# Final x by token: turned in quarters beside the second feed-forward's output products, its place lent to four raw weight buffers

## The chip, the core and the metric

The kernel runs on one core of one Trainium2 chip. The time is device microseconds (us) of one launch. Engines in the rows: PE is TensorE, DVE VectorE, ACT ScalarE, POOL GpSimd, and SP the engine whose queue issues nearly all loads.

## The reference

One encoder layer over 256 tokens of width D = 2048, in float32: two feed-forwards of width F = 5632 around a mixer and a cross-attention, and a last RMSNorm:

```python
x = x + 0.5 * swiglu_ffn(rms_norm(x, ffn1_norm), ffn1_w_in, ffn1_w_out)
...
x = x + memory_cross_attention(h, mem_n, w_q, w_kv, w_o)
x = x + 0.5 * swiglu_ffn(rms_norm(x, ffn2_norm), ffn2_w_in, ffn2_w_out)
return rms_norm(x, final_norm)          # swiglu_ffn: (silu(h @ gate) * (h @ up)) @ w_out
```

## The kernel before

**Precision and weights.** A product in float32 is made of three matmuls on a high and a low part of each operand. A weight block of 128 x 1024 floats (512 KB) is loaded by SP into a raw buffer; ACT casts it to its high part, DVE subtracts to get the low part, and PE uses both. In the feed-forward's input products ACT's cast is L341 and DVE's subtraction L342 (`parts`); elsewhere they are L112 and L113 (`weights`). The two parts of a block live in one of five places in turn (three tiles `hl`, two of `ring`), so ACT and DVE can be at most five blocks ahead of PE there, and three ahead elsewhere.

**Input products of a feed-forward (`FeedForward`, L299).** The hidden width is cut into 11 groups of 512. Group 0 is plain: 16 blocks k, each with 12 matmuls (`by_two`, L279). Groups 1 to 10 (`group`, L423) take the 16 blocks in 8 pairs: "S" pairs save one of eight products by sums of blocks (`seven`, L381, whose sums are DVE's L387, L388, L393 and L400), "C" pairs are plain (`eight`). Three blocks of a group (k = 2, 7, 13) have their low part made by an accumulating DMA that POOL issues (`summed`, L354, tile `hl_s`) instead of by DVE. At the end of a group DVE adds up what is in PSUM (L452), and `give` (L414) makes silu(gate) * up: ACT's L417, then DVE's L419. ACT's L417 therefore marks the end of each group in the trace.

**Raw buffers.** `raw` (L347) takes them in turn: four of the pool `wraw`, then those in the list `raws`. In the first feed-forward `raws` has five places, all in the tile `spare`: nine buffers in all. In the second, the first half of `spare` is `x2`, the place of the final x by token, so `raws` has one place and there are five buffers. DVE turns x (`xT`, by feature) into `x2` with 32 transpositions of 32 x 512 elements (`turn`, L973 to L981; DVE's L978), which are put on a list and issued behind DVE's subtractions during groups 0 to 2: `put(cost, ...)` appends to the list, `beside(per)` issues from it until a budget is spent. Before group 3 `then` is called (L471): it issues what is left, and four raw buffers are opened in the place of `xT`, which nobody needs any longer. From there on the second feed-forward has nine buffers too.

**Output products (`gemm_n`, L160).** The output is made in four quarters of 512 columns, each in 22 steps. A step takes one raw buffer and is 12 matmuls (L171 to L173: two blocks k, two token tiles, three matmuls each). During the first quarter the hidden tiles are also turned (`turns`, PE's L263, ACT's L120, DVE's L121). After each quarter `add_up` (L1009) adds half of the product to `x2`, and POOL multiplies by the last norm's gain; the last quarter and the norm follow at L1047 to L1074.

**What sets the order.** Within an engine a scheduler orders the instructions by a model of their times when the program is built; every engine then works its own list strictly in order, and SP's list of loads likewise. A load waits until its buffer has been read by all readers of its last contents: ACT, DVE, and for a `summed` block the DMA that POOL issued.

Of the kernel before, what the change touches and what calls it, by code (L numbers as in the profile page):

```python
# [17 lines left out]
P = 128  # L18
# [48 lines left out]
def layer(ctx: ExitStack, tc: tile.TileContext, a: dict):  # L67
# [231 lines left out]
    class FeedForward:  # L299
# [6 lines left out]
        def __init__(self, stack, tags, x_hl, gain, w_in, pattern):  # L306
# [18 lines left out]
            self.sums = spare[:, 4096:5120]  # L325
            self.raws = [spare[:, 5120:6144]]
            if tags[0] == "S1":
                self.raws += [spare[:, i * 1024:(i + 1) * 1024] for i in range(4)]
            self.raw_at = 0
# [92 lines left out]

        def group(self, j, r, per, after=()):  # L423
            b = {}
# [9 lines left out]
            for p, c in enumerate(self.pattern):  # L434
# [8 lines left out]
                else:  # L443
                    late = p > self.spairs[-1] and len(after) > 0
                    self.eight(j, p, b, p == self.pattern.index("C"), p == n - 1, late)
                    if p > self.spairs[-1] + 1:
                        for _ in range(2):
                            if after:
                                after.pop(0)()
                beside(per)  # L450
            for acc, u in (("2", p1), ("4", u2), ("3", u4), ("8", u5)):
                nc.vector.tensor_tensor(out=u, in0=u, in1=b[acc], op=ALU.add)  # L452
            self.give(j, (p1, u2), (u4, u5), r)

        def run(self, before, after, root, then, per):
            acc = token_accs()
            self.sums_at = [(j, k) for j in range(1, NG) for k in SUMMED if j < NG - 1 or k < SUMMED[-1]]
            for k in range(KD):
                before(k)
                w = self.parts(self.raw(0, k))  # L460
                begin = [(t, g) for t in range(2) for g in range(2)] if k == 0 else []
                by_two(acc, self.x_hl[:, k], w[:, 0], w[:, 1], k, begin, k == KD - 1)
                after(k)
                if k == 13:
                    r = root()
                    nc.scalar.activation(out=st.tile([P, 1], F32, name="warm"), in_=ones[:, 0:1], func=AF.Silu)
                    self.summed(*self.sums_at[0])
            self.give(0, [acc[t][0] for t in range(2)], [acc[t][1] for t in range(2)], r)
            turns = [self.turn(i) for i in range(2 * NG)]
            for j in range(1, NG):  # L470
                if j == 3:  # L471
                    then()
                if j < NG - 1:
                    self.group(j, r, per)
                else:
                    now, turns = turns[:4], turns[4:]
                    self.group(j, r, per, now)
            return turns
# [46 lines left out]
    with ExitStack() as stack:  # L525
# [21 lines left out]

        turns = ff.run(x_arrives, x_more, x_root, lambda: None, 0.0)

# [419 lines left out]
    with ExitStack() as stack:  # L969
        ff = FeedForward(stack, ("S0", "S1", "S2"), x_hl, "ffn2_norm", a["ffn2_w_in"], PATTERNS[1])  # L970
        x2 = ff.x2

        def turn(i, j):  # L973

            def go():
                q = j % 4
                dst = x2[32 * q:32 * q + 32, j // 4].rearrange("p (f n) -> p f n", n=P)
                nc.vector.transpose(  # L978
                    out=dst[:, :, 32 * i:32 * i + 32], in_=xT[32 * i:32 * i + 32, :, 32 * j:32 * j + 32]
                )  # L980
            return go  # L981

        h = ff.of
        put(0.6, *[turn(i, j) for i in range(4) for j in range(8)])

        def first_beside(k):
            if k in (6, 9, 12):
                ff.sides(k // 3 - 2)
            beside(0.8)

        def x_turned():
            finish()
            raws = xt.tile([P, 4, 1024], F32, name="raws", tag="x")
            ff.raws += [raws[:, i] for i in range(4)]

        turns = ff.run(lambda k: None, first_beside, lambda: rms_cols(ss, D, "r_x2"), x_turned, 0.6)
        finish()
        acc_0 = gemm_n(a["ffn2_w_out"][0], h, between=turns, after=0)
        ff.high.close()
# [39 lines left out]
        for n in range(3):  # L1039
            acc = gemm_n(a["ffn2_w_out"][n], h) if n else acc_0  # L1040
            for t in range(2):
                add_up(t, slice(n * 512, (n + 1) * 512), acc[t], n)


# [92 lines left out]
```

## Time and profile before

| | us |
|---|---|
| median of 3 runs (lowest, highest) | 2136.71 (2135.22, 2139.54) |
| the profiled execution, its own time | 2133.17 |
| its span, first to last instruction | 2131.4 |
| granted TensorE clock, mean of the span | 0.995 |

Times in rows are counted from the start of the span. The first feed-forward's input products take the span's first 480 us, the second's lie from 1388 to 1872 us, and its output products from 1872 us to the end. A row of the timeline gives start, duration, engine, line, operation, what it writes and reads, and in brackets for how long its engine sat idle before it and what ended that; "SPq" is SP's queue of loads, where the duration runs from the first issue to the last.

### The profile page before, as it was taken

To read this page: it belongs to the slowest core of one execution; us is meant where nothing else is said; L and a number is where in the kernel's file an instruction comes from. 1 tells how busy PE (TensorE), PEld (TensorE's weight loads), DVE (VectorE), ACT (ScalarE), POOL (GpSimd) and SP (SyncE) were. 2 spreads that over 40 slices of the span, in tenths; PEclk is the share of its full clock that TensorE was granted. 3 is DMA by queue.
4 is the path that set the end of the run, shared out by engine and by line. 5 is a ranking of instruction groups with operands and counts; after the bars stand their busy time and mean duration, and the time that the engine had idled before them with its cause. 6 is when DMAs were issued, how large, how long until landed. Compare 5 with 4: busy or idle time off the path is not lost. (4 is left out here: it accounts for less than half of the span.)

```text
span 2131.4 us, 26548 instructions
## 1 busy us (share of the span) xinstructions
PE 2091.1 (98%) x9764; PEld 1739.2 (82%) x9764; DVE 1559.3 (73%) x2119; ACT 1153.5 (54%) x1450; POOL 63.9 (3%) x81
## 2 busy tenths in 40 slices
PE   8999999999999999999999999998999999999998
PEld 6887888888888888888888888886788778888886
DVE  6887888776655589888877666797777888765444
ACT  7655566555544454445754455554565566554443
POOL 0000000000000000000000000000000000000000
PEclk9999999999999999999999999999999999999999
DMA  9787778855766766666655544566788778656664
GB/s 349 218 240 227 240 236 242 254 159 169 220 191 188 222 223 201 180 186 180 187 193 185 185 153 129 192 201 195 238 242 236 232 233 257 188 157 203 191 194 149
DMA packets 121954, 440.23 MB, mean 207 GB/s; under 512 B 13664, under 2 KB 13792, under 8 KB 121696
## 3 DMA queue, kind: packets, MB, share of 16 engines
q1 hardware_dynamic: 113184, 407.35, 59.6%
q0 software_dynamic: 8352, 30.41, 7.7%
q8 instruction: 76, 1.25, 0.2%
q10 hardware_dynamic: 288, 0.79, 0.1%
q14 instruction: 54, 0.44, 0.1%
HBM read 405.99 MB, written 2.10 MB: 191 GB/s over the span
## 5 line engine op out<-in xcount | busy, mean ns | idle before, releaser
L113 DVE TENSOR_TENSOR hl<-raw,hl 128x1024 fp32r<-128x1024 f32 (+1 forms) x402 | 489.8, 1219 | 322.1 <-ACT hl L112 321.2
L112 ACT CAST hl<-raw 128x1024 fp32r<-128x1024 f32 (+1 forms) x402 | 419.5, 1045 | 485.9 <-PE acc L173 299.7
L288 PE MATMUL acc<-hl,x_hl 128*128 128x512 f32 x440 | 151.6, 395 | 15.1 <-ACT hl L341 15.1
L341 ACT CAST hl<-spare 128x1024 fp32r<-128x1024 f32 (+1 forms) x105 | 102.8, 999 | 107.5 <-DVE spare L388 69.3
L342 DVE TENSOR_TENSOR hl<-raw,hl 128x1024 fp32r<-128x1024 f32 (+1 forms) x115 | 130.2, 1137 | 40.1 <-ACT hl L341 39.7
L289 PE MATMUL acc<-hl,x_hl 128*128 128x512 f32 x440 | 158.3, 395 | 0.1
L341 ACT CAST hl<-raw 128x1024 fp32r<-128x1024 f32 (+1 forms) x115 | 111.3, 981 | 71.6 <-DVE raw L400 40.8
L291 PE MATMUL acc<-hl,x_hl 128*128 128x512 f32 x440 | 137.9, 393 | 0.0
L342 DVE TENSOR_TENSOR hl<-spare,hl 128x1024 fp32r<-128x1024 f32 (+1 forms) x105 | 120.7, 1159 | 21.2 <-ACT hl L341 21.0
L341 ACT CAST ring<-spare 128x1024 fp32r<-128x1024 f32 (+1 forms) x75 | 74.1, 996 | 68.7 <-DVE spare L388 43.5
L288 PEld LDWEIGHTS acc<-hl,x_hl 128*128 128x128 f32 x440 | 83.5, 191 | 33.2 <-ACT hl L341 15.9
L172 PE MATMUL acc<-hl,x_hl 128*128 128x512 f32 x256 | 100.5, 392 | 0.1
L172 PE MATMUL acc<-hl,m_hl 128*128 128x512 f32 x256 | 100.3, 392 | 0.0
L173 PE MATMUL acc<-hl,m_hl 128*128 128x512 f32 x256 | 100.2, 391 | 0.0
L173 PE MATMUL acc<-hl,x_hl 128*128 128x512 f32 x256 | 99.8, 390 | 0.0
L289 PEld LDWEIGHTS acc<-hl,x_hl 128*128 128x128 f32 x440 | 83.3, 190 | 18.6 <-DVE hl L342 1.5
L291 PEld LDWEIGHTS acc<-hl,x_hl 128*128 128x128 f32 x440 | 83.7, 190 | 17.7
L342 DVE TENSOR_TENSOR ring<-spare,ring 128x1024 fp32r<-128x1024 f32 (+1 forms) x75 | 86.3, 1156 | 11.4 <-ACT ring L341 11.4
L289 PE MATMUL acc<-ring,x_hl 128*128 128x512 f32 x256 | 92.0, 390 | 2.1 <-DVE ring L342 2.1
L289 PE MATMUL acc<-hl_s,x_hl 128*128 128x512 f32 x232 | 89.3, 390 | 2.2 <-DMA hl_s<-raw 1.7
L171 PE MATMUL acc<-hl,m_hl 128*128 128x512 f32 x256 | 91.2, 392 | 0.0
L125 PE MATMUL acc<-x_hl,hl 128*128 128x512 f32 x256 | 91.0, 398 | 0.0
(343 smaller groups left out, 5185.4 us busy)
## 6 DMA issues: line engine op xcount, KB each, us to landing
raw<-in_ffn_w_in SPq DMA_DIRECT2D x176, 512.0 KB, 4.8
raw<-in_ffn_w_out SPq DMA_DIRECT2D x176, 512.0 KB, 3.8
spare<-in_ffn_w_in SPq DMA_DIRECT2D x120, 512.0 KB, 5.1
raws<-in_ffn_w_in SPq DMA_DIRECT2D x56, 512.0 KB, 5.1
raw<-in_w_mix_vg SPq DMA_DIRECT2D x32, 512.0 KB, 4.6
raw<-in_w_k SPq DMA_DIRECT2D x32, 512.0 KB, 3.9
raw<-in_w_v SPq DMA_DIRECT2D x32, 512.0 KB, 4.3
raw<-in_w_mix_out SPq DMA_DIRECT2D x32, 512.0 KB, 3.8
```

Source lines behind the costliest of these rows:

```text
L112: nc.scalar.copy(out=hl[:, 0, :size], in_=raw[:, :size])
L113: newest[0] = nc.vector.tensor_tensor(out=hl[:, 1, :size], in0=raw[:, :size], in1=hl[:, 0, :size].bitcast(F32), op=ALU.subtract)
L125: nc.tensor.matmul(acc, lhsT=w_hi, rhs=x_hl, start=first, stop=False, skip_group_check=True)
L171: nc.tensor.matmul(acc[t], lhsT=x[:, 0, s], rhs=hi[:, k], start=k0 + k == 0, stop=False)
L172: nc.tensor.matmul(acc[t], lhsT=x[:, 0, s], rhs=lo[:, k], start=False, stop=False)
L173: nc.tensor.matmul(acc[t], lhsT=x[:, 1, s], rhs=hi[:, k], start=False, stop=k0 + k == nk - 1)
L288: nc.tensor.matmul(acc[t][g], lhsT=x[:, 0, s], rhs=hi[:, cols[g]], start=(t, g) in first, stop=False)
L289: nc.tensor.matmul(acc[t][g], lhsT=x[:, 0, s], rhs=lo[:, cols[g]], start=False, stop=False)
L291: nc.tensor.matmul(acc[t][g], lhsT=x[:, 1, s], rhs=hi[:, cols[g]], start=False, stop=last)
L341: nc.scalar.copy(out=hl[:, 0, :n], in_=raw[:, :n])
L342: newest[0] = nc.vector.tensor_tensor(out=hl[:, 1, :n], in0=raw[:, :n], in1=hl[:, 0, :n].bitcast(F32), op=ALU.subtract)
```

## The change

The final x by token is no longer turned during groups 0 to 2 of the second feed-forward but during its output products, in four quarters of 512 columns: 32 transpositions of 32 x 128 elements per quarter. The first quarter's go behind the steps of the first quarter of the output, the other 96 behind the steps of the second and third. The first half of `spare` holds four raw buffers from group 0 on in both feed-forwards, and the four in the place of `xT` are gone. The calls of `beside` in the groups go with it.

```diff
@@ -323,9 +323,7 @@
             self.x2 = spare[:, :4096].rearrange("p (t d) -> p t d", t=2)
             self.free = spare[:, 4096:]
             self.sums = spare[:, 4096:5120]
-            self.raws = [spare[:, 5120:6144]]
-            if tags[0] == "S1":
-                self.raws += [spare[:, i * 1024:(i + 1) * 1024] for i in range(4)]
+            self.raws = [spare[:, i * 1024:(i + 1) * 1024] for i in (5, 0, 1, 2, 3)]
             self.raw_at = 0
...
@@ -420,7 +418,7 @@
-        def group(self, j, r, per, after=()):
+        def group(self, j, r, after=()):
...
                         for _ in range(2):
                             if after:
                                 after.pop(0)()
-                beside(per)
...
-        def run(self, before, after, root, then, per):
+        def run(self, before, after, root):
...
             for j in range(1, NG):
-                if j == 3:
-                    then()
                 if j < NG - 1:
-                    self.group(j, r, per)
+                    self.group(j, r)
...
@@ -970,32 +965,26 @@
-        def turn(i, j):
+        def turn(n, i, j):
 
             def go():
                 q = j % 4
-                dst = x2[32 * q:32 * q + 32, j // 4].rearrange("p (f n) -> p f n", n=P)
+                dst = x2[32 * q:32 * q + 32, j // 4, n * 512:(n + 1) * 512].rearrange("p (f n) -> p f n", n=P)
                 nc.vector.transpose(
-                    out=dst[:, :, 32 * i:32 * i + 32], in_=xT[32 * i:32 * i + 32, :, 32 * j:32 * j + 32]
+                    out=dst[:, :, 32 * i:32 * i + 32],
+                    in_=xT[32 * i:32 * i + 32, 4 * n:4 * n + 4, 32 * j:32 * j + 32],
                 )
             return go
 
         h = ff.of
-        put(0.6, *[turn(i, j) for i in range(4) for j in range(8)])
-
         def first_beside(k):
             if k in (6, 9, 12):
                 ff.sides(k // 3 - 2)
-            beside(0.8)
-
-        def x_turned():
-            finish()
-            raws = xt.tile([P, 4, 1024], F32, name="raws", tag="x")
-            ff.raws += [raws[:, i] for i in range(4)]
-
-        turns = ff.run(lambda k: None, first_beside, lambda: rms_cols(ss, D, "r_x2"), x_turned, 0.6)
+
+        turns = ff.run(lambda k: None, first_beside, lambda: rms_cols(ss, D, "r_x2"))
+        put(0.3, *[turn(0, i, j) for i in range(4) for j in range(8)])
+        acc_0 = gemm_n(a["ffn2_w_out"][0], h, per=0.55, between=turns, after=0)
         finish()
-        acc_0 = gemm_n(a["ffn2_w_out"][0], h, between=turns, after=0)
         ff.high.close()
...
         for n in range(3):
-            acc = gemm_n(a["ffn2_w_out"][n], h) if n else acc_0
+            if n == 1:
+                put(0.3, *[turn(m, i, j) for m in range(1, 4) for i in range(4) for j in range(8)])
+            acc = gemm_n(a["ffn2_w_out"][n], h, per=0.75) if n else acc_0
             for t in range(2):
                 add_up(t, slice(n * 512, (n + 1) * 512), acc[t], n)
+        finish()
```

Engine orders follow, the rows of each program apart; the changed program's line numbers are lower by up to 11.

SP's list of loads from the start of the second feed-forward, before. `raw` is a buffer of `wraw`, `spare` one in that tile; a row's x says how many follow each other.

```order
L351 DMA raw<-in_ffn_w_in 128x1024 x6
L351 DMA spare<-in_ffn_w_in 128x1024
L351 DMA raw<-in_ffn_w_in 128x1024 x3
L351 DMA spare<-in_ffn_w_in 128x1024
L351 DMA raw<-in_ffn_w_in 128x1024 x3
```

The same place now.

```order
L349 DMA raw<-in_ffn_w_in 128x1024 x6
L349 DMA spare<-in_ffn_w_in 128x1024 x5
L349 DMA raw<-in_ffn_w_in 128x1024 x2
L349 DMA spare<-in_ffn_w_in 128x1024 x5
L349 DMA raw<-in_ffn_w_in 128x1024 x3
```

Behind the first six loads five go into `spare` in a row where there was one, and again five after two more.

DVE's list at the end of group 0 and the start of group 1 of the second feed-forward, before: `h_11114` is group 0's result, L203 to L208 compute `r_x`, the scale of the norm by token, L342 are the subtractions.

```order
L342 TENSOR_TENSOR hl<-spare,hl 128x1024
L342 TENSOR_TENSOR hl<-raw,hl 128x1024
L387 TENSOR_TENSOR spare<-raw 128x512
L342 TENSOR_TENSOR ring<-raw,ring 128x1024
L400 TENSOR_TENSOR raw<-raw 128x512
L419 SCALAR_TENSOR_TENSOR h_11114<-acc,r_x_11409,h_11114 128x512
L342 TENSOR_TENSOR ring<-raw,ring 128x512
L978 STREAM_TRANSPOSE spare<-xT 32x16x32
L419 SCALAR_TENSOR_TENSOR h_11114<-acc,r_x_11409,h_11114 128x512
```

The same place now.

```order
L391 TENSOR_TENSOR raw<-spare 128x512
L203 TENSOR_SCALAR rv_11387<-aux 128x2
L340 TENSOR_TENSOR ring<-raw,ring 128x1024
L205 RECIPROCAL r_x_11386<-rt_11388 128x2
L398 TENSOR_TENSOR raw<-raw,spare 128x512
L206 TENSOR_TENSOR rt_11388<-r_x_11386 128x2
L207 SCALAR_TENSOR_TENSOR rt_11388<-rt_11388,rv_11387 128x2
L208 SCALAR_TENSOR_TENSOR r_x_11386<-rt_11388,r_x_11386 128x2
L340 TENSOR_TENSOR ring<-raw,ring 128x512
L417 SCALAR_TENSOR_TENSOR h_11114<-acc,r_x_11386,h_11114 128x512 x2
```

The transpositions are gone from between the subtractions. The scale by token, which before stood some thirty rows earlier, now stands just ahead of group 0's result, behind a sum of group 1's second S pair (L391).

DVE's list around the second quarter of the output products, before: L113 are the steps' subtractions, L1010 the addition to `x2`.

```order
L113 TENSOR_TENSOR hl<-raw,hl 128x1024 x2
L1010 SCALAR_TENSOR_TENSOR spare<-acc,spare 128x512 x2
L113 TENSOR_TENSOR hl<-raw,hl 128x1024 x22
L1010 SCALAR_TENSOR_TENSOR spare<-acc,spare 128x512 x2
L113 TENSOR_TENSOR hl<-raw,hl 128x1024 x22
```

The same place now.

```order
L973 STREAM_TRANSPOSE spare<-xT 32x4x32 x3
L113 TENSOR_TENSOR hl<-raw,hl 128x1024
L973 STREAM_TRANSPOSE spare<-xT 32x4x32 x3
L999 SCALAR_TENSOR_TENSOR spare<-acc,spare 128x512 x2
L113 TENSOR_TENSOR hl<-raw,hl 128x1024
L973 STREAM_TRANSPOSE spare<-xT 32x4x32 x2
L113 TENSOR_TENSOR hl<-raw,hl 128x1024
```

Two or three small transpositions now stand behind each step's subtraction.

## Rows read from the trace of the kernel before

**Rows 1.** From the page: the engines' busy time over the span, PE's busy tenths in 40 equal slices of the span, and the granted TensorE clock in the same slices.

```profile
PE 2091.1 (98%) x9764; PEld 1739.2 (82%) x9764; DVE 1559.3 (73%) x2119; ACT 1153.5 (54%) x1450; POOL 63.9 (3%) x81
...
PE   8999999999999999999999999998999999999998
...
PEclk9999999999999999999999999999999999999999
```

**Rows 2.** The timeline of ACT, the lines of L417 that mark the end of groups 0, 3 and 10, of the first feed-forward and then of the second.

```profile
54.81 1.27 ACT L417 ACTIVATE h<-acc,r_x 128x512 f32<-128x512 f32 x2
97.84 0.72 ACT L417 ACTIVATE h<-spare,r_x 128x512 f32<-128x512 f32 x1 [1.36 <-DVE spare L452]
183.37 0.72 ACT L417 ACTIVATE h<-spare,r_x 128x512 f32<-128x512 f32 x1 [1.35 <-DVE spare L452]
475.80 0.73 ACT L417 ACTIVATE h<-spare,r_x 128x512 f32<-128x512 f32 x1 [0.80 <-DVE spare L452]
1433.42 0.69 ACT L417 ACTIVATE h<-acc,r_x 128x512 f32<-128x512 f32 x1
1578.34 0.72 ACT L417 ACTIVATE h<-spare,r_x 128x512 f32<-128x512 f32 x1
1871.42 0.72 ACT L417 ACTIVATE h<-spare,r_x 128x512 f32<-128x512 f32 x1 [0.80 <-DVE spare L452]
```

**Rows 3.** Busy time in chosen stretches: groups 1 and 2 of the first feed-forward, and the same two of the second. Columns: stretch; its length and PE's busy time, then the busy times of PEld, DVE, ACT and POOL, each with its count of instructions; granted clock; DMA share; GB/s.

```profile
54.80:97.80 43.00, 43.00 (x191) 35.63 (x190) 34.29 (x42) 25.32 (x28) 2.61 (x3) 1.00 0.73 219
97.80:140.50 42.70, 42.70 (x190) 35.28 (x188) 34.25 (x43) 25.48 (x28) 2.58 (x3) 1.00 0.77 234
...
1433.40:1484.90 51.50, 43.94 (x181) 35.00 (x180) 39.04 (x47) 25.01 (x29) 2.61 (x3) 0.90 0.63 181
1484.90:1536.00 51.10, 46.61 (x197) 37.58 (x196) 39.82 (x50) 26.56 (x30) 2.62 (x3) 0.97 0.79 240
```

**Rows 4.** What PE, DVE and SP's queue waited for from 1433 to 1541 us: us in total, times, longest.

```profile
PE acc L288 <- ACT hl L341: 7.2, 1, 7.2
PE acc L275 <- ACT hl L341: 3.0, 2, 2.6
PE acc L289 <- DMA hl_s<-raw: 1.7, 1, 1.7
...
DVE spare L388 <- DMA raw<-in_ffn_w_in: 5.3, 2, 2.9
...
SPq L351 <- DMA hl_s<-raw: 31.3, 4, 11.9
SPq L351 <- DVE hl L342: 26.5, 10, 6.4
```

**Rows 5.** The timeline of all engines around PE's longest wait in group 1.

```profile
1449.89 11.79 SPq L351 DMA_DIRECT2D raw<-in_ffn_w_in  x5
1466.15 1.04 ACT L341 CAST ring<-raw 128x1024 fp32r<-128x1024 f32 x1 [6.18 <-DMA raw<-in_ffn_w_in]
1466.90 0.33 SPq L351 DMA_DIRECT2D spare<-in_ffn_w_in  x1
1471.99 2.07 PE L288 MATMUL acc<-hl,x_hl 128*128 128x512 f32 x4 [7.18 <-ACT hl L341]
```

**Rows 6.** The timeline of DVE: two steps of the first output quarter, and two of the second.

```profile
1889.33 1.23 DVE L113 TENSOR_TENSOR hl<-raw,hl 128x1024 fp32r<-128x1024 f32 x1 [1.36 <-ACT hl L112]
1890.48 0.68 DVE L121 TENSOR_TENSOR hA<-aux,hA 128x512 fp32r<-128x512 f32 x1
1892.53 1.23 DVE L113 TENSOR_TENSOR hl<-raw,hl 128x1024 fp32r<-128x1024 f32 x1 [1.37 <-ACT hl L112]
...
1961.76 1.23 DVE L113 TENSOR_TENSOR hl<-raw,hl 128x1024 fp32r<-128x1024 f32 x1 [1.49 <-ACT hl L112]
1964.48 1.22 DVE L113 TENSOR_TENSOR hl<-raw,hl 128x1024 fp32r<-128x1024 f32 x1 [1.49 <-ACT hl L112]
```

**Rows 7.** The timeline around the start of group 0 of the second feed-forward: a load into `spare`, DVE's first transpositions, and the wait of PE that follows.

```profile
1389.09 0.89 SPq L351 DMA_DIRECT2D spare<-in_ffn_w_in  x1
1391.86 4.27 DVE L978 STREAM_TRANSPOSE spare<-xT 32x512 f32<-32x512 f32 x6
1394.05 1.05 ACT L341 CAST ring<-spare 128x1024 fp32r<-128x1024 f32 x1 [1.00 <-DMA spare<-in_ffn_w_in]
1400.21 1.22 DVE L342 TENSOR_TENSOR ring<-spare,ring 128x1024 fp32r<-128x1024 f32 x1
1401.49 0.73 PE L289 MATMUL acc<-ring,x_hl 128*128 128x512 f32 x2 [0.68 <-DVE ring L342]
```

**Rows 8.** The transpositions (L978), and DVE's instruction on 128 elements per partition (L373): count, duration in ns shortest/median/longest, first and last start.

```profile
L978 DVE STREAM_TRANSPOSE spare<-xT x32: 693/703/707, 1391.9 to 1490.6; 32x512 f32<-32x512 f32 x32
...
L373 DVE TENSOR_TENSOR spare<-spare x6: 283/284/289, 5.2 to 1420.0; 128x128 f32<-128x128 f32 x6
```

**Rows 9.** ACT's part of the scale by token (its table load and its square root) in group 0 of the second feed-forward, and its work on group 0's result from PSUM.

```profile
1407.43 1.28 ACT L204 ACT_TABLE_LOAD   x1
1409.34 0.20 ACT L204 ACTIVATE rt<-rv 128x2 f32<-128x2 f32 x1 [0.62 <-DVE rv L203]
...
L417 ACT ACTIVATE h<-acc,r_x x4: 681/686/690, 54.8 to 1435.7; 128x512 f32<-128x512 f32 x4
```

More of the change, by code (lines that the diff above doesn't have):

```diff
@@ L470, in run @@
             for j in range(1, NG):
-                if j == 3:
-                    then()
                 if j < NG - 1:
-                    self.group(j, r, per)
+                    self.group(j, r)
                 else:
                     now, turns = turns[:4], turns[4:]
-                    self.group(j, r, per, now)
+                    self.group(j, r, now)
             return turns
@@ L546, in x_root @@
             return r_x
-        turns = ff.run(x_arrives, x_more, x_root, lambda: None, 0.0)
+        turns = ff.run(x_arrives, x_more, x_root)
         sm = st.tile([P, T], F32, name="sm")
```

## The prediction

> **What bounds the kernel now.** I read the page first: PE is busy for 2091 of 2131 us, nearly all forty slices read 9 or more, and the granted clock is in the highest tenth throughout [rows 1]. So a change can gain only where PE idles or is slowed, and adds time only if it makes PE wait. The one low slice inside a stage stands where the second feed-forward's first groups lie.
>
> The same feed-forward runs twice, so the first is a control for the second. The lines of ACT's L417 give the ends of groups [rows 2]. From group 0's end to group 3's the first takes 183.37 - 54.81 = 128.56 us, the second 1578.34 - 1433.42 = 144.92 us. From group 3's end to group 10's they take 475.80 - 183.37 = 292.43 and 1871.42 - 1578.34 = 293.08 us: alike. The difference, 16.36 us, lies in groups 1 and 2 alone (in group 3 both have nine raw buffers). [...]
>
> What PE waits for there ends at the raw buffers. PE's list of waits names ACT's casts (7.2 and 3.0 us) and an accumulated block (1.7); one step further back DVE waits for loads, and SP's queue is held for 31.3 us by accumulating DMAs that still read a buffer and for 26.5 us by DVE's subtractions [rows 4]. The longest case shows it in order [rows 5]: SP spreads five loads over 11.79 us because each needs a buffer back; ACT stands 6.18 us for one of them; the next load is issued at 1466.90 only; PE, out of parts, idles 7.18 us and then takes 2.07 us for four matmuls, 0.52 each, where a step of twelve lasts 2.72 later on [rows 6], 0.23 each. It is not bandwidth: that group moved 181 GB/s at a DMA share of 0.63, the first feed-forward's same group 219 at 0.73.
>
> **The change part by part.** The sum is made against the profiled execution, 2133.17 us, which is its span of 2131.4 and 1.77 around it.
>
> *Nine buffers from group 0 on.* SP's new order shows five loads into `spare` in a row where there was one, so the change does what it says, and DVE's order in groups 1 and 2 becomes almost that of the first feed-forward. Its groups are the price: -16.36 us, clock included. What is late next is what is late there, and PE did not idle in those two groups.
>
> *Group 0.* Before, six transpositions (4.27 us) and more of them stand between DVE's subtractions, the subtraction of a block in `spare` ends after 1401.4, and PE waits 0.68 us for it [rows 7]. With them gone that wait goes: -0.68. The five loads into `spare` still wait for the attention's last reader. Of the one at 1389.09 the cast began at 1394.05, and PE asked for the low part at 1401.49 - 0.68 = 1400.81 [rows 7]. At 234 GB/s, as in the first feed-forward's second group [rows 3], 512 KB take 2.24 us, less than PE takes for a block (twelve matmuls, 2.72 us as in rows 6), so loads that arrive one after another keep ahead: cost 0, which I take, since the row shows the first one 7 us early. If all five landed together, at 1389.09 + 5 x 2.24 = 1400.3, the first would be cast and subtracted by 1402.6, 1.8 us late; that is the other end.
>
> *The turn.* Removed: 32 x 0.703 = 22.5 us of DVE [rows 8], hidden except for the 0.68. Added: 128 transpositions of a quarter of the length. No row has one. Below, a quarter of 703 is 176 ns; above, 703, since nothing makes a smaller one dearer; nearest is DVE's instruction on the same 128 elements per partition, 284 ns [rows 8], and I take 0.29 us: 37 us in all. Cover: in the second and third quarter a step lasts 1964.48 - 1961.76 = 2.72 us, DVE's subtraction 1.23 of it, and it waits 1.49 us for ACT [rows 6]; 2.5 transpositions per step are 0.73. In the first quarter a step lasts 3.20 us, DVE has 1.23 + 0.68 and 1.36 idle [rows 6]; 32 in about 17.5 steps, 1.83 per step, are 0.53. What is queued behind them is the next subtraction, which waits for ACT longer than that anyway. Cost 0. At 703 ns the second and third quarter would need 1.23 + 2.5 x 0.703 = 2.99 us per step, 0.27 too much over 38.4 steps: +10.4 us.
>
> [...]
>
> *The scale by token.* It now stands in DVE's list just ahead of group 0's result, whose PSUM banks PE wants back. Counted from the end of PE's block 13, behind which its sum over features stands, ACT has a cast (1.05 [rows 5]), the table load (1.28) and the root (0.20 [rows 9]), DVE one instruction on 512 elements (0.68, as L121 in rows 6) and four small ones (no more than 0.284 each [rows 8]), and ACT again a table load (1.28, taken as the other) and 0.69 for the first bank [rows 9]: 6.3 us. Meanwhile PE has blocks 14 and 15 and then twelve matmuls of group 1 before it needs that bank, 3 x 2.72 = 8.2 us. Cost 0, with 1.9 us to spare; the first feed-forward has its scale earlier and from other data, so here the control is weakest.
>
> *Sum.* -16.36 - 0.68 = -17.0 us: 2116.1 for an execution like the profiled one. The median of the runs shown is 3.54 us above that execution, so 2136.7 - 17.0 = 2119.7 us.
>
> **The rivals.**
>
> *The scale is late.* For it: it stands behind sums that wait for loads. Against it: the 1.9 us. A wait there as long as the one of 7.18 us costs what that one did, a group of 51.5 instead of 43.0: 8.5 us given back, 2128.2.
>
> *The buffers are not it.* If groups 1 and 2 were slow for another reason (a rate of loading after group 0, say), only the 0.68 goes: 2136.0. For it: the stretch follows the attention, where the first feed-forward follows nothing. Against it: the GB/s above, and that group 3, the first with nine buffers, is at once 42.3 us long (1578.34 - 1536.0, the end of the second window [rows 2, 3]).
>
> *DVE becomes the bound in the output products.* The place is the output quarters, the price a transposition's length X. Beyond 0.60 us the 38.4 steps of the second and third quarter lose 2.5 X - 1.49 each, beyond 0.705 the 17.5 of the first 1.83 X - 1.29 each; the gain of 17.0 is gone at X = 0.756, and from there on it is slower: at 0.9 us it is 128 x 0.9 - 79.8 - 17.0 = +18.4, 2155.1. For it: a piece of 32 x 4 x 32 has four short runs, and no row shows one. Against it: 703 ns for four times as much.
>
> **How the numbers follow.** The forecast has 0.82, with 2114.5 to 2124 as its own range (the profiled execution's 2116.1 and group times that vary by a us or two); the late scale 0.05, the other reason 0.05, DVE as the bound 0.08, half of it slower, a quarter within 0.2% (4.3 us, about what a measurement of this kernel can tell from no change), a quarter still faster. Faster: 0.82 + 0.05 + 0.02 = 0.89; same 0.05 + 0.02 = 0.07; slower 0.04. The range takes in the late scale: 2114.5 to 2128.5.
>
> **What would show it.** Right: the two groups 42 to 43.5 us long at full clock; PE's list of waits from group 0 to group 3 without the 7.2; no wait of 0.68 in group 0; transpositions of about 0.29 us; steps of 2.72 and 3.20 us as before. Wrong: a wait of PE at the end of group 0 for the banks; loads into `spare` landing after 1400; DVE without idle time in the output quarters and steps longer than 2.8 us; groups 1 and 2 still at 51 us.

## The result, and the profile after

The changed kernel takes 2115.05 us (median of four runs, 2113.83 to 2118.76), the kernel before, on the same chip, 2137.2; the ratio is 0.9899, 95% interval 0.9882 to 0.9916. Run again beside three experiments (e0_again, below) the ratio was 0.9915 (0.9894 to 0.9935). The forecast was 2119.7, with a range of 2114.5 to 2128.5. The profiled execution took 2113.83 us with a span of 2111.8, so against the profiled execution of before it gained 19.34 us where the sum of the prediction said 17.0.

From the page of the changed kernel, the lines that answer to [rows 1]: PE is busy 6.5 us less, in a span that is 19.6 us shorter.

```profile
PE 2084.6 (99%) x9764; PEld 1737.2 (82%) x9764; DVE 1576.2 (75%) x2215; ACT 1156.1 (55%) x1450; POOL 66.4 (3%) x81
...
PE   8999999999999999999999999999999999999998
...
PEclk9999999999999999999999999999999999999999
```

The ends of groups 0, 3 and 10 of the second feed-forward, now ACT's L415 (start, duration; answers to [rows 2]). Group 0's end to group 3's is 1559.97 - 1433.72 = 126.25 us, where it was 144.92; group 3's to group 10's is 292.12, where it was 293.08.

```profile
1433.72 1.27 ACT L415 ACTIVATE h<-acc,r_x 128x512 f32<-128x512 f32 x2
...
1559.97 0.72 ACT L415 ACTIVATE h<-spare,r_x 128x512 f32<-128x512 f32 x1 [1.36 <-DVE spare L449]
...
1852.09 0.72 ACT L415 ACTIVATE h<-spare,r_x 128x512 f32<-128x512 f32 x1 [0.80 <-DVE spare L449]
```

The windows of its groups 1 and 2, with the columns of [rows 3]: 43.1 and 42.2 us at full clock with PE busy throughout, where they were 51.5 and 51.1.

```profile
1433.70:1476.80 43.10, 43.10 (x192) 35.71 (x191) 32.89 (x39) 25.53 (x29) 2.60 (x3) 1.00 0.72 218
1476.80:1519.00 42.20, 42.20 (x187) 34.94 (x187) 34.26 (x42) 25.02 (x29) 2.61 (x3) 1.00 0.80 238
```

What SP's queue waited for in groups 1 and 2, from 1433 to 1524 us (answers to [rows 4]). The accumulating DMAs hold it for 9.7 + 9.1 = 18.8 us, where it was 31.3 and another 7.5 on blocks in `spare`; the subtractions into `hl` for 11.4 instead of 26.5. The queue still waits, now most of all for the sums of the S pairs (L398: 26.4 us on `spare`), but the list of PE's waits from 1388 to 1560 us has no line at all.

```profile
SPq L349 <- DVE spare L398: 26.4, 5, 8.5
SPq L349 <- DVE hl L340: 11.4, 4, 3.7
...
SPq L349 <- DMA hl_s<-raw: 9.7, 3, 6.0
SPq L349 <- DMA hl_s<-spare: 9.1, 3, 4.0
```

SP's five loads into `spare` in group 0 (answers to [rows 7], where one was issued at 1389.09). The last is issued at 1393.53 and lands at 1401.76, the one before it at 1400.48. So two land after 1400, which the prediction named as a sign of being wrong, and yet PE waits for none.

```profile
1390.73 3.43 SPq L349 DMA_DIRECT2D spare<-in_ffn_w_in  x5
```

The small transpositions, and DVE's steps in the first and second output quarter (answers to [rows 6] and [rows 8]). One takes 303 ns; the steps are still 1882.81 - 1879.61 = 3.20 and 1934.28 - 1931.56 = 2.72 us, and in the steps shown DVE still waits for ACT: 0.60 us in the first quarter, 0.52 and 0.85 in the second.

```profile
L973 DVE STREAM_TRANSPOSE spare<-xT x128: 292/303/309, 1849.0 to 2020.5; 32x128 f32<-32x128 f32 x128
...
1879.61 1.23 DVE L113 TENSOR_TENSOR hl<-raw,hl 128x1024 fp32r<-128x1024 f32 x1 [0.60 <-ACT hl L112]
1880.87 0.62 DVE L973 STREAM_TRANSPOSE spare<-xT 32x128 f32<-32x128 f32 x2
1881.52 0.69 DVE L121 TENSOR_TENSOR hB<-aux,hB 128x512 fp32r<-128x512 f32 x1
1882.81 1.23 DVE L113 TENSOR_TENSOR hl<-raw,hl 128x1024 fp32r<-128x1024 f32 x1 [0.60 <-ACT hl L112]
...
1931.56 1.23 DVE L113 TENSOR_TENSOR hl<-raw,hl 128x1024 fp32r<-128x1024 f32 x1 [0.85 <-ACT hl L112]
1932.82 0.94 DVE L973 STREAM_TRANSPOSE spare<-xT 32x128 f32<-32x128 f32 x3
1934.28 1.23 DVE L113 TENSOR_TENSOR hl<-raw,hl 128x1024 fp32r<-128x1024 f32 x1 [0.52 <-ACT hl L112]
```

The scale by token at the end of group 0 (answers to [rows 9]): PE's sum over features (L232), ACT's table load and its reading of the first two banks (L415), and PE's first matmul of group 1 (L275) and its thirteenth.

```profile
1428.12 0.50 PE L232 MATMUL aux<-ones,ss 128*128 128x1 f32 x4
...
1432.42 1.28 ACT L415 ACT_TABLE_LOAD   x1
1433.72 1.27 ACT L415 ACTIVATE h<-acc,r_x 128x512 f32<-128x512 f32 x2
...
1434.02 0.39 PE L275 MATMUL acc<-hl,ring 128*128 128x512 f32 x1
...
1436.74 0.39 PE L275 MATMUL acc<-ring,x_hl 128*128 128x512 f32 x1
```

The sum starts at 1428.12, ACT begins on the banks at 1433.72 and has read the first 0.69 us later, at 1434.4; PE's thirteenth matmul of group 1 starts at 1436.74, in step. Some 2.3 us are left, where the prediction had 1.9.

Where the time went is seen best by three stretches: from PE's first matmul of the second feed-forward to group 0's end, on to group 3's, and on to group 10's. Columns: stretch; length and PE's busy time with matmuls; granted clock; DMA share; GB/s. First before, then after.

```profile
1388.49:1433.42 44.93, 44.25 (x199) 1.00 0.68 211
1433.42:1578.34 144.92, 132.78 (x562) 0.95 0.72 217
1578.34:1871.42 293.08, 289.29 (x1275) 1.00 0.77 228
```

```profile
1390.02:1433.72 43.70, 43.70 (x197) 1.00 0.77 269
1433.72:1559.97 126.25, 126.25 (x559) 1.00 0.78 233
1559.97:1852.09 292.12, 289.96 (x1282) 1.00 0.76 228
```

Altogether 482.93 us became 462.07: by these marks 1.23 us in group 0, 18.67 in groups 1 to 3, 0.96 in the rest. Of the 20.86 us, 14.45 are idle time of PE (16.61 before, 2.16 now). The other 6.41 are busy time, and the clock granted in the middle stretch rose from 0.95 to 1.00; in the trace of before it is 0.50 in the 2.11 us from 1471.99 us on, just behind PE's longest wait. The output products did not change: from group 10's end to the start of the last addition to `x2` it is 2122.02 - 1871.42 = 250.60 us before and 2102.70 - 1852.09 = 250.61 now. The second feed-forward began 1.53 us later than before (1390.02 against 1388.49), which no part of the change touches.

The marks are ACT's, and they don't stand at the same matmul of PE before and after: group 3's mark follows the 757th matmul of the stage before and the 752nd now. Counted by matmuls, whose starts are in PE's timeline, the account is sharper. The 201st, just behind group 0, starts 45.77 us after the first before and 44.91 now; the 758th, about a dozen into group 4, 189.95 and 171.16. So group 0 gained 0.86 us, groups 1 to 3 gained 144.18 - 126.25 = 17.93, and 2.07 us are gained behind them.

### The profile page after: what moved, and what is told of

The parts are those of the page before. It is cut to its first block, busy times and chain, and to the rows that moved or that the text cites. A ratio compares the mean times of both kernels' runs of the same rounds, so it can differ in the third digit from the quotient of the medians.

```text
span 2111.8 us, 26657 instructions
## 1 busy us (share of the span) xinstructions
PE 2084.6 (99%) x9764; PEld 1737.2 (82%) x9764; DVE 1576.2 (75%) x2215; ACT 1156.1 (55%) x1450; POOL 66.4 (3%) x81
## 4 chain that ended last, share of the span: by engine, by line
PE 70%; issue 25%; DMA 2%; DVE 2%; POOL 1%; ACT 1%; POOLq 0%; SPq 0%; DVEq 0%; ACTq 0%
PE acc L172 12%; PE acc L173 12%; PE acc L171 12%; PE acc L125 8%; PE acc L126 4%; PE acc L288 4%; PE acc L289 4%; PE acc L291 4%; PE aux L263 1%; PE acc L275 1%; PE acc L277 1%; PE acc L276 1%; DMA raw<-in_ffn_w_in 1%; POOL hl_s L357 1%; PE acc L1049 1%
## 5 line engine op out<-in xcount | busy, mean ns | idle before, releaser
L113 DVE TENSOR_TENSOR hl<-raw,hl 128x1024 fp32r<-128x1024 f32 (+1 forms) x402 | 489.0, 1217 | 280.9 <-ACT hl L112 279.8
L112 ACT CAST hl<-raw 128x1024 fp32r<-128x1024 f32 (+1 forms) x402 | 419.6, 1045 | 482.6 <-PE acc L173 300.1
L339 ACT CAST hl<-spare 128x1024 fp32r<-128x1024 f32 (+1 forms) x148 | 143.7, 996 | 117.0 <-DVE spare L386 55.0
L340 DVE TENSOR_TENSOR hl<-spare,hl 128x1024 fp32r<-128x1024 f32 (+1 forms) x148 | 169.7, 1158 | 32.8 <-ACT hl L339 32.2
L339 ACT CAST ring<-spare 128x1024 fp32r<-128x1024 f32 (+1 forms) x106 | 103.3, 983 | 97.7 <-DVE spare L386 49.8
L340 DVE TENSOR_TENSOR hl<-raw,hl 128x1024 fp32r<-128x1024 f32 (+1 forms) x106 | 119.6, 1133 | 47.7 <-ACT hl L339 47.0
L339 ACT CAST hl<-raw 128x1024 fp32r<-128x1024 f32 (+1 forms) x106 | 101.9, 975 | 65.4 <-DVE raw L398 27.6
L340 DVE TENSOR_TENSOR ring<-spare,ring 128x1024 fp32r<-128x1024 f32 (+1 forms) x106 | 120.4, 1142 | 21.3 <-ACT ring L339 20.8
L125 PE MATMUL acc<-y_hl,hl 128*128 128x512 f32 x256 | 90.5, 399 | 0.0
```

What stands on the lines that cost most here:

```text
L112: nc.scalar.copy(out=hl[:, 0, :size], in_=raw[:, :size])
L113: newest[0] = nc.vector.tensor_tensor(out=hl[:, 1, :size], in0=raw[:, :size], in1=hl[:, 0, :size].bitcast(F32), op=ALU.subtract)
L125: nc.tensor.matmul(acc, lhsT=w_hi, rhs=x_hl, start=first, stop=False, skip_group_check=True)
L339: nc.scalar.copy(out=hl[:, 0, :n], in_=raw[:, :n])
L340: newest[0] = nc.vector.tensor_tensor(out=hl[:, 1, :n], in0=raw[:, :n], in1=hl[:, 0, :n].bitcast(F32), op=ALU.subtract)
```

## The experiments

The table has, for each run, its median and ratio to the kernel before on the same chip, the length of the second feed-forward's input products from PE's first matmul to group 10's end in its trace, the part of it up to the start of PE's 758th matmul (groups 0 to 3 and the first few of group 4), and from group 10's end to the start of the last addition to `x2` (the output products).

| run | median us | ratio (95%) | input products | to matmul 758 | output products |
|---|---|---|---|---|---|
| before | 2137.2 | | 482.93 | 189.95 | 250.60 |
| changed | 2115.05 | 0.9899 (0.9882, 0.9916) | 462.07 | 171.16 | 250.61 |
| e0_again | 2116.75 | 0.9915 (0.9894, 0.9935) | 463.12 | 171.16 | 250.61 |
| e1_five | 2134.98 | 1.0000 (0.9988, 1.0012) | 484.48 | 189.05 | 250.61 |
| e2_early_too | 2122.72 | 0.9946 (0.9931, 0.9960) | 469.25 | 176.87 | 250.62 |
| e3_no_turn | 2115.03 | 0.9906 (0.9887, 0.9924) | 463.14 | 171.18 | 250.60 |
| e4_double | 2123.44 | 0.9959 (0.9944, 0.9974) | 461.05 | 171.16 | 259.21 |
| e5_triple | 2162.54 | 1.0142 (1.0118, 1.0166) | 465.12 | 171.14 | 295.07 |
| e6_whole | 2113.91 | 0.9926 (0.9904, 0.9949) | 464.29 | 172.13 | 250.58 |
| e7_seven | 2139.29 | 1.0037 (1.0019, 1.0055) | 488.39 | 178.28 | 250.60 |
| e8_scale_late | 2122.99 | 0.9935 (0.9919, 0.9952) | 470.22 | 176.51 | 250.61 |
| e9_eight | 2124.75 | 0.9952 (0.9934, 0.9971) | 476.44 | 175.74 | 250.60 |
| e10_eleven | 2111.74 | 0.9884 (0.9865, 0.9903) | 459.20 | 171.26 | 250.61 |
| e11_spread | 2120.69 | 0.9925 (0.9908, 0.9942) | 469.79 | 174.80 | 250.62 |

The six runs whose input products are those of the changed kernel (changed, e0, e3 to e6) lie between 461.05 and 465.12, mean 463.13: that is how far this column can be trusted. Up to matmul 758 they lie between 171.14 and 172.13, mean 171.32, and nearly all of the spread is in the rest: 289.89 (e4) to 293.98 (e5), where the kernel before has 292.98.

One more thing holds for all that follows. In e0 and e3 to e6 the lists of PE and ACT in the input products are, row for row, those of the changed kernel. In the others the scheduler, which orders by a model of times, laid them otherwise. So the price of such a run is that of its edit together with its new order, and how much is the order alone was not tried.

**e0_again: the changed kernel once more.**

> The changed kernel once more, beside the three others on the same chip, so that differences of two or three us among them can be read. 2113.8 to 2116.5 us by its runs so far; in its trace no wait of PE from the start of the second feed-forward's group 0 to the end of group 2.

2116.75 us, a little above, with PE idle for no part of groups 1 and 2. It sets the scale for the next three.

**e1_five: the buffers taken away again, the turn left where it is now.**

```diff
-            self.raws = [spare[:, i * 1024:(i + 1) * 1024] for i in (5, 0, 1, 2, 3)]
+            places = [spare[:, i * 1024:(i + 1) * 1024] for i in (5, 0, 1, 2, 3)]
+            self.raws, self.more = (places, []) if tags[0] == "S1" else (places[:1], places[1:])
...
+                if j == 3:
+                    self.raws += self.more
```

> The changed kernel with five raw buffers in groups 0 to 2 of the second feed-forward, nine from group 3 on; the turn stays in the output products. Theory (the buffers held PE up): groups 1 and 2 are slow again, group 0's end to group 3's about 140 to 145 us (126.25 in the changed kernel, 144.92 before), so about 14 to 19 us slower than the changed kernel, 2129 to 2134 us. Rival (DVE's transpositions between the subtractions held the chain up): 126 to 130 us for the three groups and no more than 4 us slower than the changed kernel, up to 2119 us. If both had a share, in between, and the run says how much each.

The whole gain is gone: ratio 1.0000, group 0's end to group 3's takes 142.71 us, and matmul 758 comes at 189.05 us where it was 189.95 before. The same three stretches of this run:

```profile
1393.54:1438.74 45.20, 45.20 (x203) 1.00 0.78 259
1438.74:1581.45 142.71, 131.57 (x552) 0.96 0.68 204
1581.45:1878.02 296.57, 291.80 (x1281) 0.99 0.76 226
```

The chain of [rows 5] stands in its timeline too, in the same order, with no transposition anywhere near: SP spreads five loads over 11.10 us, the next one is issued at 1472.89 only, ACT stands 5.71 us for it, and PE idles 4.82 us.

```profile
1456.33 11.10 SPq L350 DMA_DIRECT2D raw<-in_ffn_w_in  x5
...
1472.89 0.33 SPq L350 DMA_DIRECT2D spare<-in_ffn_w_in  x1
...
1476.76 1.04 ACT L340 CAST hl<-spare 128x1024 fp32r<-128x1024 f32 x1 [5.71 <-DMA spare<-in_ffn_w_in]
...
1477.85 1.90 PE L288 MATMUL acc<-hl,x_hl 128*128 128x512 f32 x4 [4.82 <-ACT hl L340]
```

So the buffers hold PE up by themselves. The transpositions between the subtractions were not what made groups 1 and 2 long.

**e2_early_too: nine buffers, and the old transpositions besides.**

```diff
+            beside(0.8)
...
+        def extra(i, j):
+            def go():
+                q = j % 4
+                nc.vector.transpose(out=scratch[32 * q:32 * q + 32], in_=xT[32 * i:32 * i + 32, :, 32 * j:32 * j + 32])
+            return go
+
+        scratch = ff.h[10][:, 0].rearrange("p (a b) -> p a b", a=16)
+        put(0.6, *[extra(i, j) for i in range(4) for j in range(8)])
```

(With `beside(0.6)` behind each pair again, as before. Their output goes to a place that nobody reads.)

> The changed kernel with nine buffers throughout, and in groups 0 to 2 besides the 32 transpositions of 32 x 512 of the kernel before, at the same budget, into a place that nobody reads; what the kernel computes is unchanged. Theory (the buffers): PE idles 0 to 1.5 us more, 2115 to 2117 us, group 0's end to group 3's 126 to 128 us. Rival (the transpositions): 10 us or more slower than the changed kernel, 2125 us or above, the three groups at 136 us or more.

Neither: 469.25 us for the input products, 6.1 above the mean of the six, 5.6 of it by matmul 758; all four of its times lie above all four of e0. The buffers are worth most of the gain (482.93 to 469.25, with the transpositions in both), yet the transpositions are not free once the buffers are there.

```profile
1393.94:1438.42 44.48, 44.48 (x201) 1.00 0.80 260
1438.42:1570.70 132.28, 128.84 (x560) 1.00 0.74 223
1570.70:1863.19 292.49, 289.24 (x1276) 1.00 0.77 228
```

Group 1 by engines (stretch; length, PE, PEld, DVE, ACT, POOL busy): DVE is busy for 41.09 of 45.68 us, where the changed kernel's windows above have 32.89 of 43.1. 22 of the 32 stand in group 0 in this trace as in that of before, and there PE doesn't wait and loses nothing: its 201st matmul starts 44.89 us after its first (44.91 in the changed kernel). The loss comes in groups 1 and 2.

```profile
1438.42:1484.10 45.68, 44.62 (x194) 35.84 (x192) 41.09 (x51) 24.95 (x28) 2.61 (x3) 1.00 0.67 201
```

With five buffers the move of the turn brought nothing (482.93 and 484.48); with nine it brings about 6. So the two parts of the change don't add up one by one: what the transpositions cost shows only once the longer waits for buffers are gone.

**e11_spread: the same 32, spread out; in the trace three to five to a group over groups 1 to 8, and one ahead of them.**

```diff
-            beside(0.8)
...
-lambda: rms_cols(ss, D, "r_x2"), 0.6)
+lambda: rms_cols(ss, D, "r_x2"), 0.3)
```

> The run with nine buffers and 32 additional transpositions of 32 x 512 once more, with these spread over groups 1 to 9, three or four per group, in place of all in groups 0 to 2; what the kernel computes is unchanged. There they cost 6 to 7 us, with DVE busy for 41.1 of the 45.7 us of group 1 where it is 32.9 of 43.1 without them. Theory (DVE was crowded in those groups; 3.5 x 0.70 = 2.5 us more per group would leave it 36 to 37 of 42): within 2 us of the changed kernel. Rival (a transposition between the subtractions costs its share wherever it stands): 6 us or more slower again.

The theory fell by the trace: 469.79 us, 6.7 above the mean, 3.5 of it by matmul 758; behind that it is only 1.0 above the slowest of the six. The median alone wouldn't show it (its ratio is that of e6, 0.9925 and 0.9926, each on its chip). DVE is busy for no more than 38.6 us of any group's 39.3 to 44.5. So a full DVE in two groups isn't needed: 32 transpositions between the subtractions cost some 4 to 7 us, in two groups or in eight. That the cost is in proportion to their number is not shown (in e2 most of them cost nothing where they stood). The line of PE's list of waits that grew most is the one at the ends of groups, for DVE's additions: 5.5 us in all, where the changed kernel has 2.2 and the five others 1.2 to 3.1.

```profile
PE acc L275 <- DVE spare L450: 5.5, 4, 2.0
```

**e7_seven and e9_eight: fewer buffers throughout the second feed-forward; e10_eleven: two more.** The first edit is that of e7; e9 keeps one place more (`[:4]`). For eleven the places of the hidden tiles 9 and 10 are lent until group 8.

```diff
+            if tags[0] == "S0":
+                self.raws = self.raws[:3]
```

```diff
+            if tags[0] == "S0":
+                self.raws += [self.h[j].rearrange("p a n -> p (a n)") for j in (9, 10)]
...
+                if j == 8:
+                    self.raws = self.raws[:5]
```

> The changed kernel with seven raw buffers instead of nine in all groups of the second feed-forward. Theory (the loads run ahead by what buffers there are, and a buffer that an accumulating DMA still reads holds the queue for up to 12 us, over four blocks of 2.72): in between, 2 to 8 us slower than the changed kernel over ten groups. Rival (nine are more than needed): within 1.5 us of it. Other rival (each buffer counts alike): the five of them cost 16 to 18 us in two groups, so seven over ten groups 30 us or more.

> The changed kernel with eight raw buffers instead of nine in the second feed-forward. With seven its input products took 488.4 us from their start to group 10's end, with nine 462 to 463. Theory (each buffer adds about the same): about 475 us, 12 us slower than the changed kernel. Rival (with eight the queue already runs as far ahead as PE needs): 462 to 465 us, within 2 us.

> The changed kernel with eleven raw buffers in groups 0 to 7 of the second feed-forward (the places of the hidden tiles 9 and 10 lent as well) and nine from group 8 on. Theory (with nine PE waits only for DVE's additions at the ends of groups, 2 to 3 us in all, and for no load): no more than 1.5 us faster, 461 to 463 us from the start to group 10's end. Rival (loads still set the pace somewhere): 3 us or more faster.

The sums over the three stretches of the three runs, seven, eight and eleven (length, PE's busy time):

```profile
sum 488.39, PE 472.42; mean PE 157.47
```

```profile
sum 476.44, PE 466.39; mean PE 155.46
```

```profile
sum 459.20, PE 459.20; mean PE 153.07
```

Seven cost 25 us over ten groups (488.39 - 463.13), far more than the 2 to 8 that I expected and nearer to the other rival's 30; with seven over all ten groups the kernel is slower than before, which had nine from group 3 on. Eight cost 13.3, as expected from seven and nine, in a trace whose execution was the slowest of its five by 5.8 us; by the ratios (0.9952 against 0.9899 and 0.9915) it is some 8 to 11. Eleven bring another 3.9, where I had expected at most 1.5, all of it behind matmul 758: PE is then busy for all of 459.20 us and its list of waits is empty. The longest of the three waits for DVE's additions at the ends of groups in the changed kernel (2.2 us in all) shows how a load stands behind it:

```profile
1719.27 0.69 DVE L385 TENSOR_TENSOR spare<-raw 128x512 f32<-128x512 f32 x1 [4.43 <-DMA raw<-in_ffn_w_in]
...
1729.16 2.47 DVE L449 TENSOR_TENSOR spare<-spare,acc 128x512 f32<-128x512 f32 x4
...
1729.99 0.47 PE L275 MATMUL acc<-hl,x_hl 128*128 128x512 f32 x1 [1.34 <-DVE spare L449]
```

DVE stands 4.43 us for a load and then works its list, but for one gap of 0.76 us, down to the additions for which PE waits. Over the input products DVE stands 31.6 us for loads in the changed kernel. At 2111.74 us e10_eleven is the fastest version of the study; its interval overlaps with that of the changed kernel, and its lead rests on the trace.

**e3_no_turn: the turn left out.**

```diff
-        put(0.3, *[turn(0, i, j) for i in range(4) for j in range(8)])
...
-                put(0.3, *[turn(m, i, j) for m in range(1, 4) for i in range(4) for j in range(8)])
```

> The changed kernel with the turn of x left out altogether (the final x by token isn't made, so the output is that of an unturned x). Theory (the 128 small transpositions lie in DVE's idle time): the same as the changed kernel within 1.5 us, 2114 to 2116.5 us, output steps of 2.72 and 3.20 us. Rival (they cost something on the path): more than 3 us faster, below 2112 us.

2115.03 us, and output products of 250.60 us as with the turn: the 128 small transpositions cost nothing where they stand. (The kernel leaves the turn out, so its output is that of an unturned x.)

**e4_double and e5_triple: each small transposition twice, three times (`range(3)`).**

```diff
-                nc.vector.transpose(
+                for _ in range(2):
+                    nc.vector.transpose(
```

> The changed kernel with every small transposition issued twice in a row (the second writes the same again). In the changed kernel three of them take 0.96 us of DVE and two 0.64, so 0.32 each with what lies between. Theory (a cover of 1.49 us per step in the second and third quarter, of 1.29 in the first): per transposition of the plan X = 0.64, so 38.4 x (2.5 x 0.64 - 1.49) = 4 us more than the changed kernel, about 2120 us, steps of 2.8 to 2.85 us in the second quarter, nothing in the first. Rival (DVE's work in the output products costs PE something from the first instruction on): 8 us or more. Other rival (buffers ahead take up the lateness): within 1.5 us of the changed kernel.

> The same with every small transposition issued three times, X = 0.96. Theory: 128 x 0.96 - 79.8 = 43 us more than the changed kernel (35 in the second and third quarter, 8 in the first), about 2158 us, steps of about 3.6 us in the second quarter. Rival (something besides DVE's own time counts, the clock say): 55 us or more. Other rival (the lateness is taken up elsewhere): under 30 us.

Triple: 295.07 - 250.61 = 44.5 us more in the output products, where 43 were expected. Double: 8.6 more instead of 4. That lies in the range of the rival in which every instruction of DVE costs PE something, but e3, where taking away 128 of them changed nothing, speaks against it. DVE's list in its second quarter shows why:

```profile
1964.11 1.22 DVE L113 TENSOR_TENSOR hl<-raw,hl 128x1024 fp32r<-128x1024 f32 x1
1965.36 1.30 DVE L974 STREAM_TRANSPOSE spare<-xT 32x128 f32<-32x128 f32 x4
1966.70 1.23 DVE L113 TENSOR_TENSOR hl<-raw,hl 128x1024 fp32r<-128x1024 f32 x1
1967.95 1.97 DVE L974 STREAM_TRANSPOSE spare<-xT 32x128 f32<-32x128 f32 x6
1969.96 1.23 DVE L113 TENSOR_TENSOR hl<-raw,hl 128x1024 fp32r<-128x1024 f32 x1
```

Two steps take 1969.96 - 1964.11 = 5.85 us, 2.925 each, all of it DVE's and none of it waiting: twice 1.26 for a subtraction (with 0.03 to the next instruction), and ten transpositions at 0.333. That is 0.205 above 2.72, and times 38.4 steps it is 7.9 us. The cover is 2.72 - 1.26 = 1.46 us per step, not 1.49, and a transposition in a full DVE takes 0.333 with its gap, not 0.32; close to the edge these two hundredths doubled the answer. The mechanism is the expected one.

**e6_whole: 32 whole transpositions behind the first quarter's steps alone.**

```diff
-        put(0.3, *[turn(0, i, j) for i in range(4) for j in range(8)])
-        acc_0 = gemm_n(a["ffn2_w_out"][0], h, per=0.55, between=turns, after=0)
+        put(0.7, *[turn(i, j) for i in range(4) for j in range(8)])
+        acc_0 = gemm_n(a["ffn2_w_out"][0], h, per=1.1, between=turns, after=0)
```

> The changed kernel with the turn in 32 whole transpositions of 32 x 512 (0.703 us each) behind the steps of the first output quarter alone, one or two per step: 22.5 us of DVE in place of 38.8, none in the later quarters. Theory (only DVE's place in the list counts, and the first quarter has 1.29 us of cover per step of 3.20): 1.45 x 0.72 = 1.04 us per step, hidden, within 1.5 us of the changed kernel. Rival (two in one step, 1.44 us, delay the next subtraction and PE with it): 2 to 5 us slower than the changed kernel.

(The second `put` goes, and a transposition is again the one of 32 x 512.) Output products of 250.58 us, ratio 0.9926 (0.9904 to 0.9949): no different. The cut into quarters isn't needed; 22.5 us of DVE do what 38.8 did.

**e8_scale_late: the scale by token two blocks later.**

```diff
-                if k == 13:
+                if k == (13 if self.tags[0] == "S1" else 15):
                     r = root()
```

> The changed kernel with the scale by token asked for behind block 15 of group 0 instead of block 13, that is 2 x 2.72 = 5.4 us later. In the changed kernel the sum over features starts at 1428.12 and ACT has read the first PSUM bank by 1434.4; PE has twelve matmuls of group 1 from 1434.02 on, to 1436.74, before it needs that bank: 2.4 us to spare. Theory (the scale was 2.4 us inside its cover): PE waits about 3 us once at the start of group 1 for ACT's reading, and the kernel is 2 to 4 us slower than the changed one. Rival (a wait there costs what the long one of before did, the clock with it): 8 us or more. Other rival (PE doesn't need that bank so soon): no wait, within 1 us.

PE's rows at the start of group 1 (the sum over features, then matmuls, with idle time in brackets), and at the start of group 2:

```profile
1431.21 0.50 PE L232 MATMUL aux<-ones,ss 128*128 128x1 f32 x4
1431.57 0.48 PE L275 MATMUL acc<-hl,ring 128*128 128x512 f32 x1
...
1435.01 0.50 PE L275 MATMUL acc<-hl,ring 128*128 128x512 f32 x1 [0.46 <-ACT hl L339]
...
1438.77 0.40 PE L288 MATMUL acc<-hl_s,x_hl 128*128 128x512 f32 x1
...
1479.77 0.47 PE L275 MATMUL acc<-hl,x_hl 128*128 128x512 f32 x1 [1.79 <-ACT ring L339]
```

From 1431.57 to 1438.77 PE does 23 matmuls, which at 2.72 / 12 = 0.227 us are 5.2: 2.0 us are lost there, behind ACT, whose casts and readings stand behind the scale. That is near the 3 us of the theory. But the input products are 7.1 us longer than the mean, 5.2 of it by matmul 758, so more was lost later, 1.79 of it at 1479.77, the start of group 2. How the lateness goes on to there was not tried. The place of the rival was right, and its price (8.5) nearer than mine (3), though not by its mechanism, one wait of 7 us; with 2.3 us to spare the changed kernel doesn't pay it.

## Why the prediction was right

*Nine buffers from group 0 on.* Right in cause and mechanism (e1, e7, e9), and so the rival in which the buffers are not it fell. The term of -16.36 us measured -18.67 by ACT's marks, and -17.93 by PE's matmuls, in the profiled run as in e0_again. The control was too slow by 1.4 us: for the same 557 matmuls it took 127.68 us in the trace of before, with a wait of 1.1 for DVE's additions at the end of group 3, where the second feed-forward now takes 126.25 without a wait. The prediction had looked for idle time of PE in groups 1 and 2 of the control alone.

*The turn's old place.* "hidden except for the 0.68" is the step that failed, though the sum came out: it was true of the kernel before, where PE waited for buffers anyway (e1: moving the turn alone brings nothing), and not of a kernel with nine buffers, where the same transpositions cost about 6 us (e2; 4 to 7 in e11). The control had no transpositions, and so its price already held what they would have cost. A raw-buffer change without the move of the turn, forecast by the same reasoning, would have been about 6 us too good.

*Group 0.* -0.68 was forecast; -1.23 came by ACT's marks and -0.86 by PE's matmuls. The mark misleads here: in e2, with the old transpositions in it, the stretch takes 44.48 us instead of 43.70, but 201 matmuls are in it instead of 197. The cause was only half right. In e2 the transpositions are back and the wait of 0.68 is not; in e1 the buffers are gone and it is not there either. So it took both, or the old order. PE did not wait for the five loads into `spare`.

*The turn's new place.* Cost 0, forecast and measured (250.60 and 250.61, e3 the same). 0.29 us was estimated for a small transposition, 0.303 measured. The extra work of turning in quarters, by that estimate 128 x 0.29 - 22.5 = 14.6 us, came to 38.8 - 22.5 = 16.3. The rival in which DVE becomes the bound was right as a formula to 4% at three times the work (e5), but its edge lies at 0.58 us per planned transposition, (2.72 - 1.26) / 2.5, not at 0.60 (e4).

*The scale by token.* Cover 8.2 us forecast, 1436.74 - 1428.12 = 8.6 found; chain 6.3 forecast, 1434.4 - 1428.12 = 6.3 found. The rival didn't come true.

*The median.* I added 3.54 us for the profiled execution of before being fast among its kind; that of the changed kernel was the fastest of its four too, by 1.2 us from the median. Of the 4.6 us by which 2119.7 was too high, 2.3 are this step and 2.3 the profiled gain: 3.8 us more in the input products than the sum said, less the 1.53 us by which the stage began later. Of the 3.8, 2.07 were gained behind group 3, where the prediction put nothing; that is no more than such traces differ by there.

## What to carry to other kernels

When the same stage runs twice with different means, compare it group by group: the difference prices the missing means before anything is built, and it holds the cost of everything else in which the two differ. What is hidden is hidden behind a certain wait: work that cost nothing beside waits of 16 us cost about 6 us once they were gone, so ask of a change that removes a wait which work it uncovers. And count load buffers by experiment: from seven to nine each was worth 12 to 13 us here by the traces, and at eleven PE never waited in the input products. When a stretch is measured between marks of one engine, count the other engine's instructions in it as well: a mark can move without that engine being late.

## What was not expected of the hardware

Four of DVE's transpositions of 128 elements per partition take 4 x 303 = 1212 ns, one of 512 takes 703. On a straight line through the two that is 1.04 ns per element and 0.17 us for each instruction (an estimate); the cut into quarters added 38.8 - 22.5 = 16.3 us of DVE.

The output products repeat to 0.04 us in the twelve traces other than those of e4 and e5, while PE's first matmul of the second feed-forward starts anywhere from 1386.68 (e6) to 1393.94 (e2) in programs whose earlier stages have the same source. Differences of a few us between runs come from there, and are better read from the stage that was changed than from the total.

Two more buffers (with the new order that came with them) removed waits that the trace put down to DVE's additions, an engine and a line that the buffers don't touch. The name in the list of waits was the last link only.
